# Output projection of a hybrid decoder layer: w_out split once and kept, token tiles one by one

## The chip, the cores and the metric

The kernel runs on one core of one Trainium2 chip. The metric is the device time of one execution, in microseconds (us). Before the change the median of three runs is 1144.28 us (1142.41 the lowest).

## What is computed

One decoder layer on x of 1024 tokens by 1024 features in float32: a token mixer (differential attention in 512 columns, a gated short convolution in the other 512), an output projection with a residual and a LayerNorm, then a gated MLP with a causal convolution of width 3, again with a residual and a LayerNorm. Around the change:

```python
cat = jnp.concatenate([attn_out, conv_out], axis=-1)      # (S, 1024)
mix = jnp.einsum('bsc,cd->bsd', cat, w_out)               # output projection
h = layer_norm(DEEPNORM_ALPHA * h + mix, ln1_g, ln1_b)    # h1
f = conv_glu(h, ffn_w_up, ffn_conv_w, ffn_conv_b, ffn_w_down)
```

## The kernel before

Every float32 matrix product runs in a rounded format: `split` (lines 57 to 64) cuts an operand into a high part (a cast on ACT, line 60) and a low part (a subtraction on DVE, or on POOL where asked, line 61), and `mm3` (66 to 71) issues three matmuls: high by high, high by low, low by high. The gated MLP and the input projections use a scheme of seven block products in place of eight; its seven right-hand operands for the MLP, made of the transposed h1, are `hb` "11", "21", "t1", "t2", "22", "t3" and "t4" (each a high and a low tile of 128 x 4 x 512). "11" and "21" come from tokens 0 to 511, "22" from the others, and t1 to t4 are sums and differences of both halves.

The output projection (lines 578 to 628) works on groups of three, three and two token tiles of 128 tokens (t0 = 0, 3, 6). In a group, the loop over eight k-blocks of 128 rows of w_out loads and splits the k-block (`weights`, 569 to 575: 20 loads of 512 KB in all, since two k-blocks are handed from one group to the next), loads and splits the matching piece of the mixer output `cat_d` (`cr`, `ch`, `cl`, 589 to 593), and issues 18 matmuls into the `op` accumulators (two PSUM banks for each token tile). At the end of a group DVE adds the residual to each tile (613). LayerNorm (`norm`, 615, and `layer_norm`, 514 to 525: statistics on DVE, a reciprocal root on POOL, two 128x1024 passes on DVE), the write of h1 and the eight 128x128 transposes of a tile (`trp`, 530) wait as `pending` and are called in the next group behind the k-blocks named by NORM_AT (lines 606 to 609), so that PE has matmuls ahead of and behind them.

For the tiles of the second half `combine` (543 to 567) takes the transposed tile from PSUM, rebuilds the old operands by adding their two parts on POOL (551), and makes t1, t2, 22, t3 and t4; the last of these is split by POOL. Then four gate blocks f are begun early (641 to 653) with products that need only "11" and "21", and what is left of the second half comes last (660). The pairs of the MLP follow from line 680 on.

The tile framework orders the instructions of each engine: a list scheduler takes the program's order as priority, and buffers of one tag (the eight PSUM banks have one tag, `b`) are handed out in the order in which their first writers stand. Each engine then runs its own list in order, and SP issues all DMAs in order.

Of the kernel before, what the change touches and what calls it, by code (L numbers as in the profile page):

```python
# [8 lines left out]
F32 = mybir.dt.float32  # L9
# [34 lines left out]
def layer_kernel(ctx: ExitStack, tc: tile.TileContext, x, xt, w_in, w_v, lam, vecs, w_out, ln, w_up, w_down, out):  # L44
# [468 lines left out]

    def layer_norm(pl, r, dst, gt, bt):
        st = pl.tile([P, 2, 6], F32, name="st", tag="st", bufs=3)
        for i in range(2):
            V.bn_stats(st[:, i, :], r[:, i * 512:(i + 1) * 512])
        mv = pl.tile([P, 2], F32, name="mv", tag="mv", bufs=3)
        V.bn_aggr(mv, st)
        ve = pl.tile([P, 1], F32, name="ve", tag="ve", bufs=3)  # L520
        G.tensor_scalar(ve, mv[:, 1:2], EPS, None, op0=ALU.add)
        rs = pl.tile([P, 1], F32, name="rs", tag="rs", bufs=3)
        G.tensor_tensor(rs, ve, mhalf, op=ALU.pow)
        V.scalar_tensor_tensor(r, r, mv[:, 0:1], gt, op0=ALU.subtract, op1=ALU.mult)
        V.scalar_tensor_tensor(dst, r, rs, bt, op0=ALU.mult, op1=ALU.add)

    def transposed(src, k0):
        ps = p8.tile([P, 4, P], F32, name="trp", tag="b", bufs=8)
        for j in range(4):
            T.transpose(ps[:, j, :], src[:, (k0 + j) * P:(k0 + j + 1) * P], ident)  # L530
        return ps

    def first_half(src, t):
        ts = slice(t * P, (t + 1) * P)
        for k0, n in ((0, "11"), (4, "21")):
            split(hb[n][0][:, :, ts], hb[n][1][:, :, ts], transposed(src, k0))

    def second_half(src, t):

        b_ = [transposed(src, k0) for k0 in (0, 4)]  # L540
        return lambda: combine(t, *b_)

    def combine(t, b12, b22):
        ts = slice((t - 4) * P, (t - 3) * P)

        def put(n, v, eng=None):
            split(hb[n][0][:, :, ts], hb[n][1][:, :, ts], v, eng=eng)

        def old(n, tag, bufs=1):
            v = cp.tile([P, 4, P], F32, name=f"o{n}", tag=tag, bufs=bufs)  # L550
            G.tensor_tensor(v, hb[n][0][:, :, ts].bitcast(F32), hb[n][1][:, :, ts].bitcast(F32), op=ALU.add)
            return v

        t1 = old("11", "tb0", 2)
        t4 = old("21", "tb2")
        V.tensor_tensor(t1, b12, t1, op=ALU.subtract)
        put("t1", t1)
        t2 = cp.tile([P, 4, P], F32, name="t2", tag="tb1")
        V.tensor_tensor(t2, b22, t1, op=ALU.subtract)
        put("t2", t2)  # L560
        put("22", b22)
        t3 = cp.tile([P, 4, P], F32, name="t3", tag="tb0", bufs=2)
        A.copy(t3, b12)
        V.tensor_tensor(t3, b22, t3, op=ALU.subtract)
        put("t3", t3)
        G.tensor_tensor(t4, t4, t2, op=ALU.subtract)
        put("t4", t4, G)

    def weights(t0, k, eng):
        raw = e0.tile([P, D], F32, name=f"wo{t0}_{k}_r", tag="wg", bufs=NWG)  # L570
        SQ.dma_start(raw, w_out[k * P:(k + 1) * P, :])
        wo = [e0.tile([P, 2, 512], F32R, name=f"wo{t0}_{k}_{d}", tag="ring", bufs=RING[0]) for d in range(2)]
        for d in range(2):
            split(wo[d][:, 0, :], wo[d][:, 1, :], raw[:, d * 512:(d + 1) * 512], eng=eng)
        return wo

    pending, late, held = [], [], {}
    for t0 in (0, 3, 6):
        tt = list(range(t0, min(t0 + 3, NT)))
        w = len(tt) * P  # L580
        acc = {(t, d): bank(f"op{t}_{d}") for t in tt for d in range(2)}
        order = K_ORDER if t0 != 3 else K_ORDER[::-1]
        for ki, k in enumerate(order):
            if ki < REUSE and t0:
                wo = held[k]
            else:
                wo = weights(t0, k, G if ki in POOL_LO and t0 == 6 else None)
            held[k] = wo
            cr = cc.tile([P, 384], F32, name="cr", tag="cr", bufs=4)
            SQ.dma_start(cr[:, :w], cat_d[k][:, t0 * P:t0 * P + w])  # L590
            ch = cc.tile([P, 384], F32R, name="ch", tag="ch", bufs=2)
            cl = cc.tile([P, 384], F32R, name="cl", tag="cl", bufs=2)
            split(ch[:, :w], cl[:, :w], cr[:, :w])
            if ki == 0:
                xr = {}
                for t in tt:
                    xr[t] = cx.tile([P, D], F32, name=f"xr{t}", tag="xr", bufs=4)
                    SQ.dma_start(xr[t], x[t * P:(t + 1) * P, :])
            if ki == 1 and t0 == 0:
                g1 = bcast_row(cp, 0, "g1")  # L600
                b1 = bcast_row(cp, 1, "b1")
            for i, t in enumerate(tt):
                s_ = slice(i * P, (i + 1) * P)
                for d in range(2):
                    mm3(acc[t, d], ch[:, s_], cl[:, s_], wo[d][:, 0, :], wo[d][:, 1, :], ki == 0, ki == 7)
            if pending and ki in NORM_AT:
                pending.pop(0)()
        while pending:
            pending.pop(0)()
        for t in tt:  # L610
            for d in range(2):
                ds_ = slice(d * 512, (d + 1) * 512)
                V.scalar_tensor_tensor(xr[t][:, ds_], xr[t][:, ds_], ALPHA, acc[t, d], op0=ALU.mult, op1=ALU.add)

        def norm(t, r):
            layer_norm(cp, r, r, g1, b1)
            SQ.dma_start(h1_d[t], r)

        def turn(t, r):
            if t < 4:  # L620
                first_half(r, t)
            elif t == 4:
                second_half(r, t)()
            else:
                late.append(second_half(r, t))

        rows_ = [(t, xr[t]) for t in tt]
        pending = [(lambda a=a: (norm(*a), turn(*a))) for a in rows_]
# [25 lines left out]
    wu0 = wload8(NF, "wg", NWG)
    s1 = gp.tile([P, 4, P], F32, name="s1_0", tag="s1", bufs=1)
    V.tensor_tensor(s1, wu0[:, 0:4, :], wu0[:, 4:8, :], op=ALU.add)
    v1 = parts(e0, s1)
    V.tensor_tensor(s1, s1, early[0][0][:, 0:4, :], op=ALU.subtract)
    ready1 = v1, s1, parts(e0, s1)
    for step in late:  # L660
        step()
# [274 lines left out]
```

## Time and profile before

| | us |
|---|---|
| median of the runs | 1144.28 |
| the profiled execution, its own time | 1145.87 |
| its span, first to last instruction | 1143.5 |
| PE busy in the span | 1090.8 |
| DVE busy | 914.4 |
| ACT busy | 522.5 |
| POOL busy | 174.6 |

The busy times say which engine has the most to do over the whole span; what the output projection is worth is read from its own stretch, which runs from 377.28 us (its first matmul) to about 517 us (the pairs of the MLP under way).

### The profile page before, as it was taken

To read this page: it belongs to the slowest core of one execution; us is meant where nothing else is said; L and a number is where in the kernel's file an instruction comes from. 1 tells how busy PE (TensorE), PEld (TensorE's weight loads), DVE (VectorE), ACT (ScalarE), POOL (GpSimd) and SP (SyncE) were. 2 spreads that over 40 slices of the span, in tenths; PEclk is the share of its full clock that TensorE was granted. 3 is DMA by queue.
4 is the path that set the end of the run, shared out by engine and by line. 5 is a ranking of instruction groups with operands and counts; after the bars stand their busy time and mean duration, and the time that the engine had idled before them with its cause. 6 is when DMAs were issued, how large, how long until landed. Compare 5 with 4: busy or idle time off the path is not lost.

```text
span 1143.5 us, 13823 instructions
## 1 busy us (share of the span) xinstructions
PE 1090.8 (95%) x4924; PEld 876.7 (77%) x4924; DVE 914.4 (80%) x1377; ACT 522.5 (46%) x980; POOL 174.6 (15%) x198
## 2 busy tenths in 40 slices
PE   7899999999999999789999999999999999899997
PEld 5676777877768888568888888888888887688885
DVE  7858889779887788998967676767677599977697
ACT  5347677377676334434433434343434243344450
POOL 4501313113032214760000000000000000000102
PEclk9899999999999999999999999999999999999999
DMA  7430121211205764423232222222222393111111
GB/s 257 136 111 26 42 82 41 86 60 47 79 28 172 263 203 164 152 74 111 94 109 75 92 74 93 74 93 73 93 74 74 121 411 139 37 62 40 38 74 73
DMA packets 50276, 118.51 MB, mean 104 GB/s; under 512 B 5024, under 2 KB 18464, under 8 KB 50208
## 3 DMA queue, kind: packets, MB, share of 16 engines
q1 hardware_dynamic: 50208, 117.64, 29.8%
q8 instruction: 38, 0.62, 0.2%
q14 instruction: 30, 0.25, 0.1%
HBM read 90.88 MB, written 26.74 MB: 103 GB/s over the span
## 4 chain that ended last, share of the span: by engine, by line
PE 67%; DVE 17%; ACT 6%; DMA 5%; POOL 3%; issue 2%; POOLq 0%; DVEq 0%; SPq 0%; ACTq 0%
PE X L71 8%; PE X L69 8%; PE X L70 8%; PE Z L70 5%; PE Z L71 5%; PE Z L69 5%; PE dx L70 3%; PE dx L71 3%; PE dx L69 3%; PE op L71 2%; PE op L70 2%; PE op L69 2%; DVE a L61 2%; PE dz L70 2%; PE dz L71 2%
## 5 line engine op out<-in xcount | busy, mean ns | idle before, releaser
L61 DVE TENSOR_TENSOR a<-s,a 128x512 fp32r<-128x512 f32 x118 | 85.4, 725 | 45.1 <-ACT a L60 44.1
L60 ACT CAST a<-s 128x512 fp32r<-128x512 f32 x118 | 73.4, 623 | 94.8 <-PE X L71 42.7
L60 ACT CAST a<-w 128x512 fp32r<-128x512 f32 x106 | 66.0, 623 | 87.4 <-PE X L71 40.7
L61 DVE TENSOR_TENSOR a<-w,a 128x512 fp32r<-128x512 f32 x102 | 71.4, 701 | 21.6 <-ACT a L60 21.2
L60 ACT CAST T<-b 128x512 fp32r<-128x512 f32 x66 | 40.7, 622 | 72.1 <-PE dz L71 35.6
L70 PE MATMUL dx<-T,S 128*128 128x512 f32 x176 | 69.8, 397 | 3.6 <-DVE T L61 3.6
L71 PE MATMUL dx<-T,S 128*128 128x512 f32 x176 | 69.4, 395 | 0.0
L69 PE MATMUL dx<-T,S 128*128 128x512 f32 x176 | 67.3, 390 | 0.0
L61 DVE TENSOR_TENSOR T<-b,T 128x512 fp32r<-128x512 f32 x66 | 45.4, 690 | 24.1 <-ACT T L60 24.1
L687 POOL MEMSET gs<- 128x2 f32 x22 | 2.2, 100 | 379.2 <-DVE t L706 379.2
L71 PE MATMUL op<-wo,cl 128*128 128x512 f32 x128 | 51.4, 402 | 4.5 <-DVE cl L61 4.5
L422 DVE TENSOR_REDUCE nm<-sc 128x1 f32<-128x128 f32 (+5 forms) x64 | 47.6, 751 | 7.6 <-PE sc L421 7.1
L69 PE MATMUL dz<-T,S 128*128 128x512 f32 x132 | 49.2, 401 | 3.8 <-ACT T L60 3.7
L70 PE MATMUL dz<-T,S 128*128 128x512 f32 x132 | 52.2, 396 | 0.0
L71 PE MATMUL dz<-T,S 128*128 128x512 f32 x132 | 51.9, 393 | 0.0
L69 PE MATMUL op<-wo,ch 128*128 128x512 f32 x128 | 51.4, 402 | 0.0
L70 PE MATMUL op<-wo,ch 128*128 128x512 f32 x128 | 51.0, 399 | 0.0
L426 ACT ACTIVATE p<-sc,nm 128x128 f32<-128x128 f32 (+5 forms) x64 | 47.6, 746 | 7.3 <-DVE p L435 4.1
L707 ACT ACTIVATE t<-t 128x1024 f32<-128x1024 f32 x22 | 23.4, 1062 | 51.2 <-DVE t L706 51.2
L344 POOL TENSOR_TENSOR me<-me,y 128x256 f32<-128x256 f32 x16 | 12.6, 786 | 217.9 <-ACT y L343 217.9
L419 PE MATMUL sc<-k,q 128*128 128x512 f32 (+2 forms) x96 | 37.2, 394 | 7.3 <-ACT p L426 6.1
L60 ACT CAST wo<-wo_r 128x512 fp32r<-128x512 f32 x40 | 24.4, 620 | 41.0 <-PE op L71 37.8
(312 smaller groups left out, 3415.3 us busy)
## 6 DMA issues: line engine op xcount, KB each, us to landing
w<-in_w_up SPq DMA_DIRECT2D x44, 512.0 KB, 3.3
b<-in_w_down SPq DMA_DIRECT2D x44, 256.0 KB, 6.8
w<-in_w_in SPq DMA_DIRECT2D x20, 512.0 KB, 3.5
wo_r<-in_w_out SPq DMA_DIRECT2D x20, 512.0 KB, 5.4
act_d<-act SPq DMA_DIRECT2D x19, 512.0 KB, 2.6
ra<-act_d SPq DMA_DIRECT2D x19, 512.0 KB, 7.1
v_d<-vs SPq DMA_DIRECT2D x16, 256.0 KB, 2.7
vhl<-v_d SPq DMA_DIRECT2D x8, 512.0 KB, 4.7
```

What stands on the lines that cost most here:

```text
L60: A.copy(hi, src)
L61: (eng or V).tensor_tensor(lo, src, hi.bitcast(F32), op=ALU.subtract)
L69: T.matmul(ps, lh, rh, start=first, stop=False, **kw)
L70: T.matmul(ps, lh, rl, start=False, stop=False, **kw)
L71: T.matmul(ps, ll, rh, start=False, stop=last, **kw)
L344: G.tensor_tensor(me, me, y, op=ALU.mult)
L419: T.matmul(sc[:, bs], q2[m][:, qs], k2[m][:, bs], start=True, stop=False)
L422: V.tensor_reduce(nm[:, m:m + 1], sc[:, :n], axis=AX.X, op=ALU.max, negate=True)
L426: A.activation(pt[:, :n], sc[:, :n], AF.Exp, bias=nm[:, m:m + 1], accum_out=sm[:, m:m + 1])
L687: G.memset(gs[:, 0:2], 0.0)
L707: A.activation(t_, t_, AF.Silu)
```

## The change

w_out is split once, in passes of 128x1024, into eight tiles that lie in the buffers of the operands t2, 22, t3 and t4, and stays there for all token tiles. The mixer output is split in two halves of 512 columns (`mixer`), whose tiles take the seven ring buffers and one of their own. Token tiles 0 to 2 run together over the k-blocks, then tiles 3 to 7 one by one, 48 matmuls each. Ahead of each of these stands the LayerNorm of the tile before, with its transposes. Operands of the second half are computed by rows, out of h1 as it was written to DRAM (`diff`, `b21`), and then transposed: t1 at once, the four others behind the four early gate blocks. POOL has no splits or sums there any more.

```diff
-POOL_LO = (2, 3, 4, 5, 6)
-REUSE = 2
-NORM_AT = (2, 3, 5)
...
-    def first_half(src, t):
...
-    def weights(t0, k, eng):
...
-    pending, late, held = [], [], {}
-    for t0 in (0, 3, 6):
...
+    def weights(i):
+        k = K_ORDER[i]
+        raw = e0.tile([P, 2, 512], F32, name=f"wo{k}_r", tag="wg", bufs=NWG)
+        SQ.dma_start(raw, w_out[k * P:(k + 1) * P, :].rearrange("p (a b) -> p a b", a=2))
+        tag = f"hb_{LATE_OPS[i // 2]}{'hl'[i % 2]}"
+        w = hop.tile([P, 4, 512], F32R, name=f"wo{k}", tag=tag)
+        split(w[:, 0:2], w[:, 2:4], raw)
+        wo[k] = w
...
+    def rows(t):
+        xr[t] = cx.tile([P, D], F32, name=f"xr{t}", tag="xr", bufs=5)
+        SQ.dma_start(xr[t], x[t * P:(t + 1) * P, :])
+        acc[t] = [bank(f"op{t}_{d}") for d in range(2)]
...
+    def first_half(t):
+        norm(t)
+        put("11", t, transposed(xr[t], 0))
+        put("21", t, transposed(xr[t], 4))
...
+    def second_half(t):
+        r = xr[t]
+        v = cx.tile([P, 512], F32, name=f"diff{t}", tag="diff", bufs=4)
+        SQ.dma_start(v, h1_d[t - 4][:, 0:512])
+        norm(t)
+        V.tensor_tensor(v, r[:, 0:512], v, op=ALU.subtract)
+        put("t1", t, transposed(v, 0))
+        V.tensor_tensor(v, r[:, 512:D], v, op=ALU.subtract)
+        diff[t] = v
+
+    def late(n, t):
+        r = xr[t]
+        if n == "t2":
+            src = diff[t]
+        elif n == "22":
+            src = r[:, 512:D]
+        elif n == "t3":
+            src = r[:, 0:512]
+            V.tensor_tensor(src, r[:, 512:D], src, op=ALU.subtract)
+        else:
+            src = cc.tile([P, 512], F32, name=f"b21_{t}", tag="cr", bufs=3)
+            SQ.dma_start(src, h1_d[t - 4][:, 512:D])
+            V.tensor_tensor(src, src, diff[t], op=ALU.subtract)
+        put(n, t, transposed(src, 0))
+
+    for t in range(3):
+        rows(t)
+    for i in range(NK):
+        weights(i)
+        mixer(i, 0)
...
+        for t in range(3):
+            mms(t, i)
+    for t in range(3, NT):
+        rows(t)
+        if t == 4:
+            for i in range(NK):
+                mixer(i, 1)
+        if t == 3:
+            for u in range(3):
+                first_half(u)
+        elif t == 4:
+            first_half(3)
+        else:
+            second_half(t - 1)
+        for i in range(NK):
+            mms(t, i)
+    second_half(NT - 1)
...
     for f in range(NEARLY):
-        if f >= NEARLY - 2:
-            turn(*rows_[f - NEARLY + 2])
...
+        for t in range(4, NT):
+            late(LATE_OPS[f], t)
```

On PE, before, around the transposes of the first token tile (`trp` is the transposed tile, `xr` the normed rows, `op` an accumulator, `wo` a part of w_out, `ch` and `cl` the parts of the mixer output; the `op` rows are of the second group of tiles):

```order
L71 MATMUL op_0_3956<-wo_6_0_4014,cl 128x512
L69 MATMUL op_1_3957<-wo_6_1_4015,ch 128x512
L70 MATMUL op_1_3957<-wo_6_1_4015,ch 128x512
L71 MATMUL op_1_3957<-wo_6_1_4015,cl 128x512
L530 MATMUL trp<-ident,xr_3694 128x128 x8
L69 MATMUL op_0_3952<-wo_2_0_4072,ch 128x512
L70 MATMUL op_0_3952<-wo_2_0_4072,ch 128x512
L71 MATMUL op_0_3952<-wo_2_0_4072,cl 128x512
```

On PE, changed, at the end of token tiles 0 to 2 (`c` is a split tile of the mixer output; `op_0_3902` belongs to tile 3):

```order
L68 MATMUL op_0_3670<-wo_3874,c_3_3879 128x512
L66 MATMUL op_1_3671<-wo_3874,c_3_3879 128x512
L67 MATMUL op_1_3671<-wo_3874,c_3_3879 128x512
L68 MATMUL op_1_3671<-wo_3874,c_3_3879 128x512
L528 MATMUL trp<-ident,xr_3660 128x128 x8
L528 MATMUL trp<-ident,xr_3664 128x128 x8
L528 MATMUL trp<-ident,xr_3668 128x128 x8
L66 MATMUL op_0_3902<-wo_3674,c_4_3679 128x512
L67 MATMUL op_0_3902<-wo_3674,c_4_3679 128x512
L68 MATMUL op_0_3902<-wo_3674,c_4_3679 128x512
```

The 24 transposes of tiles 0 to 2 now stand directly behind the matmuls that make these tiles and ahead of the first matmul of tile 3. On PE, changed, between tiles 4 and 5 (`op_1_4043` is of tile 4, `diff_4164` is made of its normed rows, `op_0_4162` is of tile 5):

```order
L66 MATMUL op_1_4043<-wo_3874,c_3_4081 128x512
L67 MATMUL op_1_4043<-wo_3874,c_3_4081 128x512
L68 MATMUL op_1_4043<-wo_3874,c_3_4081 128x512
L528 MATMUL trp<-ident,diff_4164 128x128 x4
L66 MATMUL op_0_4162<-wo_3674,c_4_4046 128x512
L67 MATMUL op_0_4162<-wo_3674,c_4_4046 128x512
L68 MATMUL op_0_4162<-wo_3674,c_4_4046 128x512
```

So it stands behind every tile from 3 to 7. On ACT, before, where the stage begins (`me` and `y` belong to the last attention output and follow the matmuls into `mq`):

```order
L60 CAST wo_4_0_3682<-wo_4_r 128x512
L60 CAST wo_4_1_3683<-wo_4_r 128x512
L60 CAST wo_5_0_3720<-wo_5_r 128x512
L60 CAST wo_5_1_3721<-wo_5_r 128x512
L60 CAST ch<-cr 128x384 x2
L60 CAST wo_0_0_3756<-wo_0_r 128x512
L60 CAST wo_0_1_3757<-wo_0_r 128x512
L60 CAST wo_1_0_3788<-wo_1_r 128x512
L340 ACTIVATE me<-mq,epsc 128x256
L342 ACTIVATE y<-me 128x256
L343 ACTIVATE y<-y 128x256
```

On ACT, changed, at the same place:

```order
L57 CAST c_4_3679<-cr 128x512
L57 CAST c_5_3707<-cr 128x512
L57 CAST c_0_3739<-cr 128x512
L337 ACTIVATE me<-mq,epsc 128x256
L57 CAST c_1_3767<-cr 128x512
L339 ACTIVATE y<-me 128x256
L340 ACTIVATE y<-y 128x256
L57 CAST c_2_3795<-cr 128x512
L57 CAST c_6_3823<-cr 128x512
L57 CAST wo_3674<-wo_r 128x1024
L57 CAST wo_3702<-wo_r 128x1024
```

The first cast of w_out, which stood ahead of the operations on `mq`, now stands behind them and behind two casts of the mixer output. DVE has the same change: the first low part of w_out stands behind the convolution's last passes (before: lines 442 to 449) and two low parts of the mixer output.

## Rows read from the trace of the kernel before

**Rows 1.** Windows of core 0: busy us (instructions) by engine, granted clock, DMA share, GB/s

```profile
449.00:482.00 33.00, 26.18 (x115) 19.50 (x114) 32.01 (x38) 16.01 (x32) 27.17 (x20) 0.96 0.47 155
482.00:518.00 36.00, 31.06 (x127) 24.69 (x126) 33.48 (x43) 14.20 (x26) 20.71 (x17) 0.90 0.16 59
518.00:536.00 18.00, 17.89 (x79) 14.50 (x78) 15.12 (x23) 10.36 (x17) 0.10 (x1) 1.00 0.37 124
...
377.28:510.36 133.08, 123.44 (x547) 98.31 (x545) 112.37 (x148) 51.26 (x99) 63.22 (x49) 0.97 0.50 170
510.36:517.55 7.19, 5.06 (x14) 3.52 (x13) 6.50 (x10) 3.45 (x6) 2.87 (x3) 0.76 0.00 0
```

**Rows 2.** What PE waited for from 377 to 518 us: total, times, longest

```profile
PE op L71 <- DVE cl L61: 4.5, 3, 2.3
...
PE trp L530 <- DVE xr L525: 2.2, 1, 2.2
```

**Rows 3.** Timeline of PE: start, us, instruction, [idle before it <- releaser]

```profile
377.28 0.40 PE L69 MATMUL op<-wo,ch 128*128 128x512 f32 x1
...
377.98 0.40 PE L69 MATMUL op<-wo,ch 128*128 128x512 f32 x1
...
423.48 1.03 PE L530 MATMUL trp<-ident,xr 128*128 128x128 f32 x8
424.27 0.48 PE L69 MATMUL op<-wo,ch 128*128 128x512 f32 x1
...
469.49 1.06 PE L530 MATMUL trp<-ident,xr 128*128 128x128 f32 x8 [2.24 <-DVE xr L525]
...
479.40 0.63 PE L70 MATMUL op<-wo,ch 128*128 128x512 f32 x1
...
481.96 0.63 PE L70 MATMUL X<-hb_11l,a 128*128 128x512 f32 x1
```

**Rows 4.** Timeline of PE in the first microseconds of the kernel

```profile
9.66 0.79 PE L69 MATMUL vps<-wv_s,xb_11h 128*128 128x512 f32 x1 [1.37 <-ACT xb_11h L60]
...
14.52 0.61 PE L70 MATMUL vps<-wv_s,xb_11h 128*128 128x512 f32 x1
```

**Rows 5.** Timeline of DVE: residual sums, statistics and the passes of LayerNorm

```profile
479.71 1.87 DVE L613 SCALAR_TENSOR_TENSOR xr<-xr,op 128x512 f32<-128x512 f32 x3
...
482.38 1.87 DVE L517 BATCH_NORM_STATS2 st<-xr 128x6 f32<-128x512 f32 x3
...
484.83 1.27 DVE L524 SCALAR_TENSOR_TENSOR xr<-xr,mv,g 128x1024 f32<-128x1024 f32 x1
486.02 0.20 DVE L519 BATCH_NORM_AGGREGATE mv<-st 128x2 f32<-128x12 f32 x1
...
486.69 2.31 DVE L525 SCALAR_TENSOR_TENSOR xr<-xr,rs,b 128x1024 f32<-128x1024 f32 x1
```

**Rows 6.** Timeline of POOL: the reciprocal root of a LayerNorm

```profile
484.75 0.57 POOL L523 TENSOR_TENSOR rs<-ve,mhalf 128x1 f32<-128x1 f32 x1
```

**Rows 7.** Groups by form: line, engine, operation, count | busy us, mean ns | idle before

```profile
L61 DVE TENSOR_TENSOR wo<-wo_r,wo 128x512 fp32r<-128x512 f32 x24 | 19.6, 822 | 10.8 <-ACT wo L60 10.8
...
L61 DVE TENSOR_TENSOR wv_s<-wv_r,wv_s 128x1024 fp32r<-128x1024 f32 x3 | 3.7, 1226 | 0.8 <-ACT wv_s L60 0.8
L60 ACT CAST wv_s<-wv_r 128x1024 fp32r<-128x1024 f32 x3 | 3.1, 1045 | 0.9 <-DMA wv_r<-in_w_v 0.8
```

**Rows 8.** Timelines of ACT and DVE where the stage begins

```profile
378.44 0.42 ACT L343 ACTIVATE y<-y 128x256 f32<-128x256 f32 x1
...
381.80 0.71 DVE L449 TENSOR_TENSOR w<-p,w 128x512 f32<-128x512 f32 x1
```

**Rows 9.** SP's queue, a window of the DMAs, and DMA groups (KB each, median us to landing)

```profile
391.61 0.33 SPq L590 DMA_DIRECT2D cr<-cat_d  x1
...
391.00:396.00 5.00, 5.00 (x23) 3.99 (x23) 2.56 (x5) 1.56 (x3) 0.00 (x0) 1.00 0.97 369
...
h_d<-xr SPq DMA_DIRECT2D x8, 512.0 KB, 4.0
```

More of the change, by code (lines that the diff above doesn't have):

```diff
@@ L503, in layer_kernel @@
     cp = pool("cp", cp_st, side="right")
-    hb = {n: [hop.tile([P, 4, 512], F32R, name=f"hb_{n}{c}", tag=f"hb_{n}{c}") for c in "hl"] for n in OPS}
+    LATE_OPS = ("t2", "22", "t3", "t4")
+    hb = {}
     def bank(name):
@@ L531, in transposed @@
         return ps
-    def first_half(src, t):
[L534 to L567, printed above, removed]
@@ L569, in weights @@
-    def weights(t0, k, eng):
-        raw = e0.tile([P, D], F32, name=f"wo{t0}_{k}_r", tag="wg", bufs=NWG)
-        SQ.dma_start(raw, w_out[k * P:(k + 1) * P, :])
-        wo = [e0.tile([P, 2, 512], F32R, name=f"wo{t0}_{k}_{d}", tag="ring", bufs=RING[0]) for d in range(2)]
-        for d in range(2):
-            split(wo[d][:, 0, :], wo[d][:, 1, :], raw[:, d * 512:(d + 1) * 512], eng=eng)
-        return wo
-    pending, late, held = [], [], {}
-    for t0 in (0, 3, 6):
[L579 to L628, printed above, removed]
@@ new lines, in put @@
+    def put(n, t, v):
+        if n not in hb:
+            hb[n] = [hop.tile([P, 4, 512], F32R, name=f"hb_{n}{c}", tag=f"hb_{n}{c}") for c in "hl"]
+        ts = slice(t % 4 * P, (t % 4 + 1) * P)
+        split(hb[n][0][:, :, ts], hb[n][1][:, :, ts], v)
+    wo = {}
+    def weights(i):
[6 more added lines that the diff above has]
+        wo[k] = w
@@ new lines, in layer_kernel, with mixer @@
+    cat = {}
+    def mixer(i, half):
+        k = K_ORDER[i]
+        cr = cc.tile([P, 512], F32, name="cr", tag="cr", bufs=3)
+        SQ.dma_start(cr, cat_d[k][:, half * 512:(half + 1) * 512])
+        if i < NK - 1:
+            c = e0.tile([P, 2, 512], F32R, name=f"c{half}_{k}", tag="ring", bufs=RING[0])
+        else:
+            c = cc.tile([P, 2, 512], F32R, name=f"c{half}_{k}", tag="c8")
+        split(c[:, 0], c[:, 1], cr)
+        cat[half, k] = c
+    xr, acc = {}, {}
+    def rows(t):
+        xr[t] = cx.tile([P, D], F32, name=f"xr{t}", tag="xr", bufs=5)
+        SQ.dma_start(xr[t], x[t * P:(t + 1) * P, :])
+        acc[t] = [bank(f"op{t}_{d}") for d in range(2)]
@@ new lines, in mms, with norm @@
+    def mms(t, i):
+        k = K_ORDER[i]
+        c, w, ts = cat[t // 4, k], wo[k], slice(t % 4 * P, (t % 4 + 1) * P)
+        for d in range(2):
+            mm3(acc[t][d], c[:, 0, ts], c[:, 1, ts], w[:, d], w[:, 2 + d], i == 0, i == NK - 1)
+    def norm(t):
+        r = xr[t]
+        for d in range(2):
+            ds_ = slice(d * 512, (d + 1) * 512)
+            V.scalar_tensor_tensor(r[:, ds_], r[:, ds_], ALPHA, acc[t][d], op0=ALU.mult, op1=ALU.add)
+        layer_norm(cp, r, r, g1, b1)
+        SQ.dma_start(h1_d[t], r)
@@ new lines, in first_half @@
+    def first_half(t):
+        norm(t)
+        put("11", t, transposed(xr[t], 0))
+        put("21", t, transposed(xr[t], 4))
+    diff = {}
+    def second_half(t):
[7 more added lines that the diff above has]
+        diff[t] = v
@@ new lines, in late @@
+    def late(n, t):
+        r = xr[t]
+        if n == "t2":
[10 more added lines that the diff above has]
+        put(n, t, transposed(src, 0))
@@ new lines, in layer_kernel @@
+    for t in range(3):
[3 more added lines that the diff above has]
+        mixer(i, 0)
+        if i == 1:
+            g1, b1 = bcast_row(cp, 0, "g1"), bcast_row(cp, 1, "b1")
+        for t in range(3):
[10 more added lines that the diff above has]
+            first_half(3)
+        else:
+            second_half(t - 1)
+        for i in range(NK):
+            mms(t, i)
@@ L631, in layer_kernel @@
+    second_half(NT - 1)
+    for n in LATE_OPS:
+        hb[n] = [hop.tile([P, 4, 512], F32R, name=f"hb_{n}{c}", tag=f"hb_{n}{c}") for c in "hl"]
     early = {}
@@ L639, in wgate @@
         return wload8(f, "wg", NWG)
-    for a in rows_:
-        norm(*a)
     for f in range(NEARLY):
-        if f >= NEARLY - 2:
-            turn(*rows_[f - NEARLY + 2])
         wg, X, Y = wgate(f), bank(f"X{f}"), bank(f"Y{f}")
@@ L649, in layer_kernel @@
         A.copy(p1, X)
-        block_product(e0, Y, None, hb, "21", True, parts(e0, wg[:, 4:8, :], G))
+        block_product(e0, Y, None, hb, "21", True, parts(e0, wg[:, 4:8, :]))
         c11 = gp.tile([P, 512], F32, name=f"c11_{f}", tag="c11", bufs=NEARLY)
@@ L653, in layer_kernel @@
         early[f] = wg, X, c11
[L654 to L661, printed above, removed]
+        if f == NEARLY - 1:
+            wu0 = wload8(NF, "wg", NWG)
+            s1 = gp.tile([P, 4, P], F32, name="s1_0", tag="s1", bufs=1)
+            V.tensor_tensor(s1, wu0[:, 0:4, :], wu0[:, 4:8, :], op=ALU.add)
+            v1 = parts(e0, s1)
+            V.tensor_tensor(s1, s1, early[0][0][:, 0:4, :], op=ALU.subtract)
+            ready1 = v1, s1, parts(e0, s1)
+        for t in range(4, NT):
+            late(LATE_OPS[f], t)
     cp_st.close()
```

## The prediction

> **What bounds the kernel now.** I read the granted clock and the span first, then windows over the stage, then what PE waited for, and last the timelines of PE and DVE at the places that the change moves. Outside the stage PE is full: from 518 to 536 us it is busy 17.89 of 18.00 us, 79 matmuls, 0.2265 us each [rows 1]. So only time in which PE gets through its list slower than that is to be won or lost.
>
> The stage runs from its first matmul at 377.28 to 517.55 us, 133.08 + 7.19 = 140.27 us [rows 1, 3]. What must be done in it: 384 matmuls of the output projection at 0.2333 us (three from 377.28 to 377.98 [rows 3]) = 89.6 us; 96 of the early gate blocks and 13 of the first pair at 0.2265 = 24.7 us; 64 transposes, of which eight and the longer matmul behind them cost 0.87 us (423.48 to 424.27, and 0.48 in place of 0.40 [rows 3]) = 7.0 us. That is 121.3 us, so 19.0 us are lost, nearly all behind 449 us, where PE is busy 26.18 of 33 and 31.06 of 36 us [rows 1]. The reader is to see there that PE waits for low parts of the mixer output (4.5 us) and for the last pass of a LayerNorm (2.2 us) [rows 2], and that behind the waits matmuls come at 0.427 us: seven from 479.40 to 481.96, in a stretch with a mean granted clock under 1 [rows 1, 3], which is the 1.2 GHz level.
>
> **What goes.** w_out is split 16 times (in units of 128x512) and not 40 times, and POOL leaves the stage. At most this gives back the 19.0 us: PE cannot be faster than full. I count it all as gained and enter below what comes in its place.
>
> **More transposes.** t1, t2, 22, t3 and t4 are transposed apart, 16 each for four tiles, so 32 + 80 = 112 in place of 64. 48 more at 0.87 / 8 = 5.2 us.
>
> **The start.** Before, w_out's first parts were ready when PE came from the projections; PE went on at 377.28 without a gap [rows 3]. Now the first cast of w_out stands behind the operations on `mq` and behind casts of the mixer output. The last operation on `mq` ended at 378.86 [rows 8]; with one more cast ahead of it and two behind, about 0.5 us each, ACT begins with w_out at 380.5 and is done at 381.6 (1.045 us [rows 7]). On DVE the low part stands behind the last convolution pass, which ended at 382.5 [rows 8] and now does so at about 381.9, and behind two low parts of 0.6 us: 383.1, and 1.23 us more [rows 7] is 384.3. PE can do two matmuls before that. Loss: 384.3 - 377.28 - 0.5 = 6.5 us. Ends: 4 us if the casts of the mixer output come early, 8 us if one of their loads is late.
>
> Later k-blocks cost nothing if they come in time. The sixth has to wait in SP's queue for the last piece of the convolution: before, the read behind it went out at 391.61 [rows 9]. Behind it now go two pieces of the mixer output, three tiles of x, two rows of LayerNorm and w_out's sixth block, 3.5 MB; at the 369 GB/s of that time [rows 9] it lands at 401 and is split by 404. PE wants it at 384.3 + 5 x 18 x 0.2333 + 2 = 407. At half the rate it would come 6 us late; I take nothing and keep 6 us for the range.
>
> **Behind tiles 0 to 2.** Here the order decides. PE's next rows are 24 transposes, which need three finished LayerNorms, and tile 3's matmuls stand behind them. Before, matmuls of the next group stood on both sides. What DVE has left when the last matmul of tile 2 is issued: some 0.5 us of a residual sum; ten operations on 128x512 (two residual sums, four statistics, four low parts) at 1.87 / 3 = 0.62; two aggregations of 0.2; six passes on 128x1024 at 1.19 (484.83 to 486.02), with POOL idle, for with a split on POOL one took 2.31 [rows 5]. 0.5 + 6.2 + 0.4 + 7.1 = 14.2 us. POOL's root (0.57 us [rows 6]) lies beside the first pass. In that time PE does 16 of the transposes, 1.7 us: 12.5 us are lost.
>
> **Behind tiles 3 to 7.** After tile 3 DVE does one residual sum, two low parts of the mixer output, two statistics, an aggregation and two passes: 0.2 + 5 x 0.62 + 0.2 + 2.4 = 5.9, with the handover 6.0 us. After tiles 4 to 7 the two low parts are not in it, but a subtraction is, the rows minus the old h1 (not in the trace in this form; the residual sum, also on 128x512, is nearest): 0.2 + 0.62 + 1.25 + 0.2 + 2.4 + 0.62 + 0.1 = 5.4 us, four times: 21.6 us. Nothing else is on PE's list in these gaps.
>
> **The clock.** Seven gaps of 5 us and more now stand before a dense stretch: the start, behind tiles 0 to 2, and behind 3, 4, 5, 6 and 7. After a wait of 2.3 us seven matmuls ran at 0.427 us, 1.35 us lost [rows 2, 3]; in the first microseconds of the kernel, after one of 1.37 us, twelve did (9.66 to 14.52 [rows 4]), 2.3 us lost. I take 2.0 us, nearer to the second since these gaps are longer: 14.0 us, with 9.5 and 16 as ends.
>
> **Late operands.** Behind each early gate block stand 16 transposes. DVE has seven operations there (4.3 us) and PE 24 matmuls and the transposes (7.2 us), so PE covers them. Only the last tile's t4 waits: its load of old h1 needs a buffer that the first tile's transposes free, and takes about as long as the write of h1, 4.0 us [rows 9], against some 3.4 us of PE's work; with the subtraction 1.0 us is lost. SP now has h1's writes ahead of the reads of old h1, each waiting for its LayerNorm; what is queued behind (rows of x, old h1) is wanted tiles later, over 15 us.
>
> **Sum.** 6.5 + 12.5 + 6.0 + 21.6 + 14.0 + 1.0 + 5.2 = 66.8 us, less 19.0: +47.8 us. The profiled execution took 1145.87 us (span 1143.5), so 1193.7; the median of the runs is 1.6 us lower: 1192 us.
>
> **Rivals.**
>
> *PE stays full.* If tile t+1's matmuls ran while the LayerNorm of tile t is going on, the gaps behind the tiles and their clock losses would fall away, and -19.0 + 5.2 + 6.5 + 2.0 = -5.3 us would be left: 1139 us, not slower. For it speaks that DVE sheds 24 splits of w_out and runs without POOL's splits, which had stretched a mean low part of w_out to 822 ns [rows 7]. It decides at the first transposes behind tile 2: either a matmul of tile 3 is issued before them or not. Against it: at 469.49 PE sat idle for 2.24 us in front of eight transposes until DVE's pass was done [rows 3], and each tile's LayerNorm takes its first number from the last matmul ahead of the gap, so no faster DVE closes it. I give it 0.04. The Trainium skill ("TensorE: Matmul & The Clock Gate", section "Step-by-step: what each phase is for") says that PE pulls only weight loads ahead and keeps matmuls in program order; by that rule this rival falls, and the idle 2.24 us agree.
>
> *Every stretch runs at the lower clock.* If, with a gap after each 48 matmuls, PE kept the 0.427 us for all of them, tiles 3 to 7 would cost 5 x 48 x 0.193 = 46 us where the sum has 10: 1228 us. For it: behind 449 us waits of some 2 us already brought the mean granted clock to 0.96, 0.90 and 0.76 [rows 1]. Against it: the last row of the slow seven is 2.6 us behind the first [rows 3], and even the kernel's first stretch was slow for some 5 us only [rows 4], less than half of the 11.2 us of a tile. 0.07. The Trainium skill (same page, section "HAM oscillation — how this bites in real kernels") shows a loop whose bursts of some 2 us start cold each time after waits of 3 to 5 us; a tile's stretch is five times as long, so by that page too the beginning alone is slow.
>
> *w_out's late blocks hold PE.* The 6 us above, twice over with the loads of x ahead of them: 1204 us, chance 0.04. Inside the range.
>
> **How the numbers follow.** The forecast, a gap behind each tile, has 0.85, and the rivals 0.04, 0.07 and 0.04. Its own ends: clock 9.5, start 4 and no wait for the last t4 give -8; clock 16, start 8 and 6 us for w_out give +10; durations of the chain on DVE, of some 40 us, 10% either way: 4 more. So 1180 to 1206; I give 1178 to 1210, which leaves out the first two rivals and a little at each end. A measurement of this kernel tells about 2% from no change, 23 us: slower by over 2% has all cases but the first rival and a little of the forecast's low end: 0.94; within 2% 0.05; faster 0.01.
>
> **What would show it.** In the changed kernel's trace: PE idle by some 12 us around its first transposes, with DVE's second pass of a LayerNorm as releaser; five more gaps of 5 to 6 us, about 19 us apart (11.2 of matmuls, 0.5 of transposes, 2 for the clock, 5.4 of waiting); the first matmul of the stage with w_out's low part at about 384; PE busy at some 70% over tiles 3 to 7, with a granted clock below 0.95; the pairs of the MLP 48 us later than before and then as before. The forecast is wrong if matmuls of a next tile stand in front of its predecessor's transposes in the trace, or if the gaps are under 3 us.

## The result, and the profile after

The changed kernel takes 1200.72 us (median; 1197.77 to 1201.74) beside 1144.03 us for the kernel before in the same comparison: ratio 1.0496, 95% interval 1.0469 to 1.0524. It is slower by 5%, inside the predicted range and 9 us above the predicted time. One of the four executions of the kernel before took 2755.74 us; the ratio leaves it out, and the median of the other three is 1143.79 us. The profiled execution took 1199.74 us (span 1198.0), 53.9 us more than that of the kernel before.

All of it lies in the stage of the output projection. The engines are PE (TensorE, the matmuls), DVE (VectorE), ACT (ScalarE) and POOL (GpSimd). The columns of a window are the stretch and its length, the busy us (and instructions) of PE, of PE's weight loads, of DVE, ACT and POOL, then the granted clock, the DMA share and GB/s. The changed kernel over tiles 4 to 7 with the four early gate blocks, over the beginning of the pairs, and over tiles 3 to 7 alone:

```profile
456.00:568.00 112.00, 86.25 (x370) 70.59 (x369) 52.59 (x77) 18.74 (x34) 7.50 (x9) 0.86 0.06 25
568.00:586.00 18.00, 17.55 (x79) 13.90 (x78) 17.24 (x26) 9.17 (x16) 0.10 (x1) 1.00 0.47 162
...
434.00:537.00 103.00, 68.28 (x264) 54.71 (x263) 49.81 (x70) 12.95 (x22) 9.36 (x11) 0.83 0.19 65
```

The second row answers to the last of the three stretches of [rows 1] (518 to 536): 79 matmuls in 18 us here and there, so the pairs run as before. In the first row every engine has time to spare: PE is busy for 77% and DVE for 47%, and the granted clock is 0.86; over tiles 3 to 7 alone it is 66%, 48% and 0.83. No engine is the bound where all of them have slack; what binds is a chain that goes from one to the other and back. What PE waited for from 376 to 575 us (total, times, longest), to be read beside [rows 2]:

```profile
PE trp L528 <- DVE diff L596: 25.8, 4, 6.7
PE trp L528 <- DVE xr L523: 19.6, 4, 9.0
PE op L66 <- ACT wo L57: 4.5, 1, 4.5
PE op L67 <- DVE wo L58: 1.7, 1, 1.7
```

These are ten gaps, 51.6 us. Before, all waits of PE there came to 11.6 us: the two groups of [rows 2], 4.5 and 2.2 us, 2.6 us in shorter ones, and this one:

```profile
PE X L69 <- ACT t L563: 2.3, 1, 2.3
```

The gaps one after the other, in the PE timeline of the changed kernel (start, duration, instruction, in brackets the idle time before it and what ended it); around 475 us some of the matmuls behind a gap are shown too:

```profile
380.27 1.22 PE L66 MATMUL op<-wo,c 128*128 128x512 f32 x2 [4.55 <-ACT wo L57]
383.20 0.80 PE L67 MATMUL op<-wo,c 128*128 128x512 f32 x1 [1.71 <-DVE wo L58]
...
421.78 1.71 PE L528 MATMUL trp<-ident,xr 128*128 128x128 f32 x8 [3.75 <-DVE xr L523]
427.23 1.97 PE L528 MATMUL trp<-ident,xr 128*128 128x128 f32 x8 [3.73 <-DVE xr L523]
432.38 1.97 PE L528 MATMUL trp<-ident,xr 128*128 128x128 f32 x8 [3.18 <-DVE xr L523]
...
454.97 1.94 PE L528 MATMUL trp<-ident,xr 128*128 128x128 f32 x8 [8.97 <-DVE xr L523]
...
475.64 1.08 PE L528 MATMUL trp<-ident,diff 128*128 128x128 f32 x4 [6.40 <-DVE diff L596]
476.38 0.78 PE L66 MATMUL op<-wo,c 128*128 128x512 f32 x1
476.95 0.63 PE L67 MATMUL op<-wo,c 128*128 128x512 f32 x1
477.38 0.63 PE L68 MATMUL op<-wo,c 128*128 128x512 f32 x1
...
480.26 0.40 PE L66 MATMUL op<-wo,c 128*128 128x512 f32 x1
480.50 0.39 PE L67 MATMUL op<-wo,c 128*128 128x512 f32 x1
480.73 0.40 PE L68 MATMUL op<-wo,c 128*128 128x512 f32 x1
```

The pattern of 475.64 comes again at 495.63, 515.89 and 536.70 (6.29, 6.31 and 6.74 us idle). From 476.95 to 479.51 the matmuls start 0.427 us apart, as those at 1.2 GHz in [rows 3]; from 480.26 on 0.24 us and less. The lower level of the clock holds for the first 4 us of each tile's stretch and not for the rest. If every start more than 0.3 us behind the one before it is counted, and what it takes beyond 0.2265 us is added up (for transposes, beyond 0.109 us, which 16 of them take in e1_within where PE is full), the ten gaps cost 20.3 us behind them: 3.3 at the start, 3.8 around the transposes of tiles 0 to 2, 2.4 to 3.1 behind each of tiles 3 to 7 (13.2). Not quite all of it is the clock: in e2_dummy below, where the clock stays up behind tiles 3 to 7, the same count still finds 1.2 us behind five gaps. So some 18 us are the clock.

With that the stage adds up. It runs from 375.7 to 571.5 us, 195.8. The 384 matmuls at 0.227 us (50 of them from 388.26 to 399.61) are 87.2; gate blocks and the first pair's beginning 24.7, as before; transposes 7.0 + 5.2; gaps 51.6; what is lost behind the gaps 20.3; together 196.0.

Why a gap behind a tile is 6.4 us long is read from DVE's timeline between tiles 4 and 5, and POOL's:

```profile
468.57 1.39 DVE L579 SCALAR_TENSOR_TENSOR xr<-xr,op 128x512 f32<-128x512 f32 x2 [10.31 <-PE op L68]
469.88 1.28 DVE L515 BATCH_NORM_STATS2 st<-xr 128x6 f32<-128x512 f32 x2
471.19 0.21 DVE L517 BATCH_NORM_AGGREGATE mv<-st 128x2 f32<-128x12 f32 x1
471.43 1.28 DVE L522 SCALAR_TENSOR_TENSOR xr<-xr,mv,g 128x1024 f32<-128x1024 f32 x1
473.48 1.28 DVE L523 SCALAR_TENSOR_TENSOR xr<-xr,rs,b 128x1024 f32<-128x1024 f32 x1 [0.76 <-POOL rs L521]
474.80 0.69 DVE L596 TENSOR_TENSOR diff<-xr,diff 128x512 f32<-128x512 f32 x1
```

```profile
418.29 0.24 POOL L519 TENSOR_SCALAR ve<-mv 128x1 f32<-128x1 f32 x1 [32.88 <-DVE mv L517]
...
471.49 1.31 POOL L519 TENSOR_SCALAR ve<-mv 128x1 f32<-128x1 f32 x1 [17.98 <-DVE mv L517]
472.88 0.57 POOL L521 TENSOR_TENSOR rs<-ve,mhalf 128x1 f32<-128x1 f32 x1
```

DVE idles 10.31 us for the tile's last matmul and then PE idles for DVE: the two take turns. Inside the chain DVE waits 0.76 us for POOL, whose addition of one number to each row takes 1.31 us here and 0.24 us at 418.29.

### The profile page after: what moved, and what is told of

The parts are those of the page before. It is cut to its first block, busy times and chain, and to the rows that moved or that the text cites. A ratio compares the mean times of both kernels' runs of the same rounds, so it can differ in the third digit from the quotient of the medians.

```text
span 1198.0 us, 13747 instructions
## 1 busy us (share of the span) xinstructions
PE 1104.2 (92%) x4972; PEld 889.0 (74%) x4972; DVE 898.3 (75%) x1359; ACT 505.3 (42%) x936; POOL 128.0 (11%) x168
## 4 chain that ended last, share of the span: by engine, by line
PE 52%; DVE 7%; DMA 4%; POOL 1%; issue 1%; ACT 0%; SPq 0%; POOLq 0%; DVEq 0%; ACTq 0%
PE X L66 7%; PE X L67 7%; PE X L68 7%; PE Z L66 3%; PE Z L68 3%; PE Z L67 3%; PE dx L67 3%; PE dx L68 3%; PE dx L66 2%; PE Y L68 2%; PE dz L68 2%; PE dz L67 2%; PE Y L67 2%; PE Y L66 2%; PE dz L66 2%; DMA h_d<-xr 1%
## 5 line engine op out<-in xcount | busy, mean ns | idle before, releaser
L58 DVE TENSOR_TENSOR a<-w,a 128x512 fp32r<-128x512 f32 x106 | 74.8, 705 | 28.9 <-ACT a L57 28.4
L66 PE MATMUL op<-wo,c 128*128 128x512 f32 x128 | 55.3, 434 | 4.5 <-ACT wo L57 4.5
L67 PE MATMUL op<-wo,c 128*128 128x512 f32 x128 | 53.9, 421 | 1.7 <-DVE wo L58 1.7
L68 PE MATMUL op<-wo,c 128*128 128x512 f32 x128 | 53.7, 419 | 0.0
L717 ACT ACTIVATE t<-t 128x1024 f32<-128x1024 f32 x22 | 23.4, 1062 | 47.8 <-DVE t L716 47.8
L67 PEld LDWEIGHTS dx<-T,S 128*128 128x128 f32 x176 | 33.4, 190 | 11.9 <-DVE T L58 4.9
L66 PEld LDWEIGHTS dx<-T,S 128*128 128x128 f32 x176 | 33.3, 189 | 7.5 <-ACT T L57 0.6
```

The costliest lines, as they stand in the source:

```text
L717: A.activation(t_, t_, AF.Silu)
```

## The experiments

The theory: the time is lost because, in PE's program order, each tile's transposes stand directly behind its own matmuls, so that PE waits through a whole LayerNorm, and then pays again in clock. The rivals: DVE, the splits of w_out, the loads or the extra transposes would cost the time in any order; or the clock costs little.

**e1_within.** Each tile's LayerNorm and transposes are called inside the matmuls of the next tile, the last tile's behind the first gate block (so that the transposes of its t2 stand one gate block later too). Nothing else is changed: the same instructions, splits and loads.

```diff
+    DUE = {3: {2: (0,), 6: (1,)}, 4: {1: (2,), 5: (3,)}, 5: {5: (4,)}, 6: {5: (5,)}, 7: {5: (6,)}}
     for t in range(3, NT):
...
-        if t == 3:
-            for u in range(3):
-                first_half(u)
-        elif t == 4:
-            first_half(3)
-        else:
-            second_half(t - 1)
         for i in range(NK):
             mms(t, i)
+            for u in DUE[t].get(i, ()):
+                (first_half if u < 4 else second_half)(u)
-    second_half(NT - 1)
...
-        for t in range(4, NT):
+        if f == 0:
+            second_half(NT - 1)
+        for t in range(4, NT - 1 if f == 0 else NT):
             late(LATE_OPS[f], t)
+        if f == 1:
+            late(LATE_OPS[0], NT - 1)
```

> The changed kernel, but each tile's LayerNorm and transposes stand among the matmuls of the next tile (behind its third to seventh k-block) and tile 7's behind the first gate block; everything else as changed. Theory (the order makes the gaps, and the gaps lower the clock): of the changed trace's 51.6 us of waits in the stage the 10.7 behind tiles 0 to 2, the 9.0 behind tile 3 and the 25.7 behind tiles 4 to 7 go, and most of some 17 us at the lower clock with them; the start (6.3 us) and 48 transposes stay: about 1200 - 45 - 13 = 1142 us, PE idle under 5 us between 384 us and the pairs. Rival (DVE, ACT or the loads bound the tiles and the order only shows it): waits turn up among the matmuls in place of the gaps, and the time stays above 1180 us.

Measured: 1145.37 us, ratio 1.001 (1.000 to 1.002). PE's waits from 376 to 530 us, and the window that stands above for the changed kernel:

```profile
PE op L66 <- ACT wo L57: 3.8, 1, 3.8
PE op L67 <- DVE wo L58: 2.4, 1, 2.4
PE trp L528 <- DVE xr L523: 2.3, 3, 1.6
PE trp L528 <- DVE diff L596: 2.3, 1, 2.3
```

```profile
456.00:568.00 112.00, 109.25 (x517) 89.34 (x516) 91.99 (x136) 42.76 (x73) 6.23 (x10) 1.00 0.21 80
```

45.4 us of waiting for LayerNorms have become 4.6, and in the same stretch of time 517 matmuls stand where 370 did (from 514.5 us on those of the pairs), at a full clock. So 55 of the 57 us came from the order alone: the calls move a tile's LayerNorm on DVE and POOL and its write of h1 along with the transposes, but not what has to be done. The time is 3 us above the expectation, which had no waits for LayerNorms left; the four short waits are of that size.

**e2_dummy.** Behind the matmuls of each of tiles 3 to 7, ahead of its transposes, 24 more matmuls into a bank of their own, whose result nobody reads. The gaps are filled with work of no use.

```diff
+    def keep(t):
+        ps = bank(f"kp{t}")
+        c, w = cat[t // 4, K_ORDER[NK - 1]], wo[K_ORDER[NK - 1]]
+        for j in range(24):
+            T.matmul(ps, c[:, 0, t % 4 * P:(t % 4 + 1) * P], w[:, j % 2], start=j == 0, stop=j == 23)
...
+        keep(t)
```

> The changed kernel with 24 more matmuls behind each of tiles 3 to 7, into a PSUM bank that nobody reads; they take 24 x 0.2333 = 5.6 us of PE in gaps of 6.3 to 9.0 us. The chain on DVE is the same. Theory (the clock falls because PE is idle, and costs about 2 us behind each gap): PE's clock stays up in tiles 4 to 7 and the kernel gets faster by 5 x 2 = 10 us, to about 1190 us, though it does 120 matmuls more. Rival (the matmuls behind a gap are slow for another reason, such as a load or the weights): no faster than the changed kernel, 1200 us, or slower if the added matmuls delay the transposes.

Measured: 1187.74 us, ratio 1.0382 (1.0366 to 1.0397): 13.0 us faster than the changed kernel with 120 matmuls more. PE between tiles 4 and 5, and the window again:

```profile
466.69 5.76 PE L620 MATMUL kp<-wo,c 128*128 128x512 f32 x24
473.18 0.66 PE L528 MATMUL trp<-ident,diff 128*128 128x128 f32 x4 [0.72 <-DVE diff L596]
473.59 0.48 PE L66 MATMUL op<-wo,c 128*128 128x512 f32 x1
```

```profile
456.00:568.00 112.00, 107.99 (x509) 88.04 (x508) 62.98 (x93) 24.54 (x45) 7.53 (x9) 1.00 0.13 48
```

Behind tiles 3 to 7 the gaps and the added matmuls take 6.0 + 27.2 = 33.2 us where the gaps alone took 34.7. What is saved is mainly the clock: counted as above, 1.2 us are lost behind these gaps and not 13.2. 1.5 + 12.0 = 13.5 us answer to the 13.0 measured, so the clock is shown to cost time apart from the gaps.

**e3_act_root.** The reciprocal root of the LayerNorm is made by ACT (a logarithm and an exponential) and not by POOL.

```diff
-        G.tensor_scalar(ve, mv[:, 1:2], EPS, None, op0=ALU.add)
+        A.activation(ve, mv[:, 1:2], AF.Ln, bias=epsc)
-        G.tensor_tensor(rs, ve, mhalf, op=ALU.pow)
+        A.activation(rs, ve, AF.Exp, scale=-0.5)
```

> The changed kernel with the reciprocal root of the first LayerNorm on ACT (Ln, then Exp with scale -0.5) in place of POOL. Theory (POOL's addition is held while DVE's first pass runs, so that the second pass waits 0.75 us for the root): the 0.75 us wait ahead of the second pass goes in tiles 3 to 7, the gaps fall from 6.4 to about 5.65 us, 5 x 0.75 = 3.8 us in all: about 1197 us. Rival (the wait is the handover itself): ACT's two operations and handovers take as long, no change within 1 us.

Measured: 1196.69 us, ratio 1.046 (1.0441 to 1.0478), 4.0 us below the changed kernel (the runs of the two just overlap, 1194.88 to 1198.34 and 1197.77 to 1201.74; the profile shows the cause more directly). DVE's two passes now stand 0.12 us apart and the four gaps behind tiles 4 to 7 are 2.6 us shorter (25.8 before):

```profile
470.15 1.28 DVE L522 SCALAR_TENSOR_TENSOR xr<-xr,mv,g 128x1024 f32<-128x1024 f32 x1
471.55 1.29 DVE L523 SCALAR_TENSOR_TENSOR xr<-xr,rs,b 128x1024 f32<-128x1024 f32 x1
```

```profile
PE trp L528 <- DVE diff L596: 23.2, 4, 6.1
```

**e4_cat_early.** The pieces of the mixer output for the second half are loaded into the buffers of w_out's loads, which stand empty, and not into the three `cr` buffers.

```diff
+        if half:
+            if i % 2 == 0:
+                crs.append(e0.tile([P, 2, 512], F32, name=f"cr{i}", tag="wg", bufs=NWG))
+            cr = crs[-1][:, i % 2, :]
...
```

> The changed kernel with the second half of the mixer output loaded into the buffers of the w_out and gate weights, all eight pieces before the first LayerNorm's write of h1 is waited for, and not through three small buffers. Theory (tile 3's gap is 9.0 us and not 6.4 since the last two pieces land late and DVE's statistics stand behind their low parts): the gap behind tile 3 falls to about 6.5 us, time 1198 us. Rival (the two low parts themselves lengthen it): it stays above 8 us.

Measured: 1198.44 us, ratio 1.048 (1.0459 to 1.0501). The gap behind tile 3 fell from 8.97 to 6.71 us. The time fell by 2.3 us as well, but its runs spread from 1195.01 to 1199.95 us, so that the time by itself would not show it. By the profile, 2.3 us of that gap were low parts of the mixer output that came late and stood ahead of the LayerNorm on DVE.

**e6_start and e5_within_start.** The first two k-blocks of w_out go into four ring buffers and four pieces of the mixer output into two buffers of t2 in their place, so that w_out's first cast can stand ahead of the operations on `mq`; e6_start is the changed kernel with this alone, e5_within_start is e1_within with it (transposes of tiles 0 to 3 one k-block later, those of tile 7 behind the second gate block).

```diff
+        if i < 2:
+            w = [e0.tile([P, 2, 512], F32R, name=f"wo{k}{c}", tag="ring", bufs=RING[0]) for c in "hl"]
+            split(w[0], w[1], raw)
...
-        if i < NK - 1:
+        if i < 3:
             c = e0.tile([P, 2, 512], F32R, name=f"c{half}_{k}", tag="ring", bufs=RING[0])
+        elif i < NK - 1:
+            if i % 2:
+                two[half, i] = hop.tile([P, 4, 512], F32R, name=f"c{half}_{k}", tag=f"hb_t2{'hl'[i // 2 - 1]}")
+            c = two[half, i - 1 + i % 2][:, 2 - i % 2 * 2:4 - i % 2 * 2]
```

> The changed kernel with the buffers of e5_within_start alone; the order behind the tiles is the changed kernel's. Theory: the start's gap of 6.3 us and some 2 us of the clock behind it go: 1200.7 - 8 = about 1192 us. Rival (the wait moves to the third k-block or is hidden by the gaps that follow): 1198 us or more.

> As e1_within, with the first two k-blocks of w_out in ring buffers and four tiles of the mixer output in their place, so that the first split of w_out can be made while the projections still run; the transposes of tiles 0 to 3 are one k-block later, those of tile 7 behind the second gate block. Theory (the stage loses by PE's gaps and by the clock behind them): the gap of 6.3 us at the start with some 2 us of the clock, and 4.6 us of waits at transposes, go: 1145.4 - 8 - 4 = about 1133 us, faster than both kernels. Rival (DVE, which then has the splits of w_out and the convolution's last passes in the same time, is the bound there, and PE waits for the third k-block instead): 1141 us or more.

Measured: e6_start 1198.36 us, ratio 1.0484 (1.0458 to 1.0509); e5_within_start 1140.66 us, ratio 0.9982 (0.9970 to 0.9995). PE goes from the projections into the stage without a gap in both, so the start's 6.3 us and its clock are gone, but only 2.4 us (within the spread of the runs) and 4.7 us of them show in the time. The theory's numbers, 1192 and 1133 us, did not come out. The rivals' times did, 1198 or more for the one and, but for 0.3 us, 1141 or more for the other; not their wait at the third k-block, which is in neither profile, but what e6_start's rival named second, that the gaps that follow hide the gain. The time went into the gap ahead of the first transposes, 3.75 us in the changed kernel, 11.0 in e6_start and 6.5 in e5_within_start, where e1_within had 0.3. PE's longest waits in e6_start, and the row of DVE's timeline that stands right ahead of tile 0's residual sums:

```profile
PE trp L528 <- DVE xr L523: 25.3, 4, 11.0
```

```profile
415.23 0.69 DVE L675 TENSOR_TENSOR s<-w 128x512 f32<-128x512 f32 x1 [10.11 <-DMA w<-in_w_up]
```

It is a sum over a block of w_up that is not needed before the pairs, and it waits 10.1 us for its load, and all LayerNorms with it. In the changed kernel the same instruction waited until 414.40, which cost little there, as the tiles themselves came late.

**e7_within_start_act.** e5_within_start with ACT's root, the edit of e3_act_root.

> e5_within_start with the reciprocal root as a logarithm and an exponential on ACT, so that DVE's second pass no longer waits 0.75 us for POOL. Theory (DVE's chain lies beside matmuls now): the same as e5_within_start within 2 us. Rival (DVE is the bound behind the tiles): 4 us or more below it.

Measured: 1141.54 us, ratio 0.9981 (0.9969 to 0.9992), the same as e5_within_start within 1 us. Where DVE's chain has matmuls beside it, POOL's delay costs nothing that these runs can tell.

**e9_start_s1 and e8_within_start_s1.** The early sum `s1` takes the buffer of `p1`, which binds it to the end of the gate blocks.

```diff
-            s1 = gp.tile([P, 4, P], F32, name="s1_0", tag="s1", bufs=1)
+            s1 = gp.tile([P, 4, P], F32, name="s1_0", tag="p1", bufs=1)
```

> e6_start with the same one buffer changed, the order behind the tiles being the changed kernel's. Theory: the first gap at the transposes falls from 11.0 us to 4 to 5 us, 1198.4 - 6.5 = about 1192 us, so that the start's loss is worth 8 us in the changed kernel once nothing takes its place. Rival: the gap stays as long, as the LayerNorms of tiles 0 to 2 need that time on DVE, 1197 us or more.

> e5_within_start with one buffer changed: s1, a sum over a block of w_up for the first pair, takes the buffer of p1, so that it stands on DVE behind the gate blocks and no longer, waiting 10.9 us for its load, ahead of tile 0's residual sums. Theory (that wait has taken over what the start gave): the 6.5 us gap at the first transposes and some 2 us of the clock behind it go: 1140.7 - 8.5 = about 1132 us. Rival (DVE is late there by its own work, or by the loads of x): 1139 us or more.

Measured: e9_start_s1 1195.26 us, ratio 1.0451 (1.0428 to 1.0474); e8_within_start_s1 1136.78 us, ratio 0.9938 (0.9920 to 0.9956). The gap at the first transposes fell to 3.42 us in the one and vanished in the other, as expected, and a part was lost again. PE's waits in e8_within_start_s1, and DVE's list there:

```profile
PE trp L528 <- DVE b L622: 3.9, 1, 3.9
PE trp L528 <- DVE xr L523: 2.0, 2, 1.6
```

```profile
499.62 0.69 DVE L670 TENSOR_TENSOR s<-w 128x512 f32<-128x512 f32 x1
...
502.63 0.68 DVE L672 TENSOR_TENSOR s<-s,w 128x512 f32<-128x512 f32 x1
503.23 0.69 DVE L622 TENSOR_TENSOR b<-b,diff 128x512 f32<-128x512 f32 x1
```

Now `s1` and its splits stand ahead of the subtraction for the last tile's t4, for which PE waits. The 3.9 us cost another 2.7 us in clock. The same wait of 3.9 us stands in e9_start_s1, with 1.7 us of clock behind it; that more than covers the 3 us by which this run misses its expectation.

**e11_within_start_s1b.** e8_within_start_s1 with two buffers for `p1` and `s1`, so that `s1` stands one gate block earlier.

> e8_within_start_s1 with two buffers for p1 and s1, so that s1 and its splits stand on DVE behind the third gate block and no longer ahead of the last tile's t4. Theory (the wait of 3.9 us before the last transposes came from that order on DVE): it goes, with some 1 us of the clock: 1136.8 - 5 = about 1132 us. Rival (the last tile's t4 waits for its load of old h1 all the same): 1135 us or more.

Measured: 1130.83 us, ratio 0.9892 (0.9874 to 0.9909): faster than the kernel before by 1.1% and than the changed one by 5.8%. All that PE waited for from 376 to 530 us, and the window from its first matmuls to the pairs:

```profile
PE trp L528 <- DVE xr L523: 2.5, 2, 1.6
```

```profile
376.00:520.00 144.00, 141.44 (x677) 117.05 (x676) 113.49 (x164) 44.59 (x77) 19.49 (x23) 1.00 0.45 160
```

So the plan of the change (w_out kept, tile by tile, sums by rows) costs 57 us with the transposes behind their own tiles, and gains 13 once they, w_out's first two k-blocks and `s1` are placed so that PE's list stays full.

## Why the prediction was right, and where its sizes were off

*What goes (19.0 us), More transposes (5.2).* Not measured apart. Together they say -13.8 us for a stage without gaps; e11_within_start_s1b, with 2.5 us of waits left, is at -12.9 against the kernel before in the same comparison. The reading of the profile before left out PE's 2.3 us of waiting for ACT; as the term takes all that PE lost, the sum is the same.

*The start (6.5).* Right: 4.55 + 1.71 = 6.3 us, with the named operations as releasers and the first use of the low part at 383.20 (384 predicted). The later k-blocks of w_out cost nothing, as taken: no other wait for `wo` stands among PE's waits.

*Behind tiles 0 to 2 (12.5).* 3.75 + 3.73 + 3.18 = 10.7 us; smaller, because the transposes between the waits ran slowly (1.97 us for eight, where 0.87 was taken) and so filled more of DVE's chain.

*Behind tiles 3 to 7 (6.0 + 21.6).* The mechanism is right and the size was 7 us short: 8.97 + 25.7 = 34.7. The step said "POOL's root (0.57 us [rows 6]) lies beside the first pass", for tiles 0 to 2, and took the two passes as 2.4 us here too. The root does not lie beside the pass: it waits for POOL's addition, which ends with the pass, and the second pass comes 0.76 us late. e3_act_root takes that away: 2.6 us over the four gaps behind tiles 4 to 7, and 0.6 of the fifth, where DVE's wait fell from 0.74 to 0.12 us. (The fifth gap fell by 1.9 us in all; the rest is no gain of the root, as tile 3's matmuls ended 1.2 us later in that run while the last low part of the mixer output stood at the same time, 449.28 and 449.35 us.) Behind tile 3 the late pieces of the mixer output are the other part, 2.3 us by e4_cat_early. What is left, some 1.6 us over four gaps, fits the last residual sum, which ends 0.7 us behind a tile's last matmul where the step took 0.2; no run changes it.

*The clock (14.0, ends 9.5 and 16).* Mis-sized as well: 20.3 us by the count above, some 18 of them the clock, beyond its upper end either way. The step took 2.0 us for each of seven gaps, from the start of the kernel; five of them cost 2.4 to 3.1, and the other two groups, which are two and three gaps in a row, 3.3 and 3.8. That it is the clock and not the gaps is shown by e2_dummy. The step's first figure came from one wait of 2.34 us (ahead of 478.04); behind the wait of 2.24 us in [rows 3] (ahead of 469.49) no matmul was slow, so that the price of a single gap was less sure than the step had it.

*Late operands (1.0).* Nothing: no wait for `b` stands in the changed kernel's profile. It is there in e8_within_start_s1 and e9_start_s1, by DVE's order and not by the load that the step named.

The errors (-0.2, -1.8, +7.1, +6.3, -1.0, and -2.4 since matmuls ran at 0.227 us and not 0.2333) sum to 8.0 us; the stage grew by 195.8 - 140.3 = 55.5 where 47.8 was forecast. In part they cancel: two terms were 13.4 us too small and the others 5.4 too large. Without those 5.4 the time would still lie in the range. The time of the whole grew by 1.6 us less, as the stage began earlier.

*The rivals.* "PE stays full" fell at the place that was named: no matmul of tile 3 is issued ahead of the first transposes. e1_within makes its condition true, and gives 1145 where it said 1139. Of the 6 us, 4.6 are the short waits, and some 1.4 the clock at the start, 3.4 us where 2.0 was taken; behind the short waits the clock stayed up. One number that spoke for this rival was misread: before, DVE made 30 and POOL 10 of the 40 low parts of w_out, and DVE now makes 16 (8 of 128x1024), so that DVE shed 14 of them and not 24. "Every stretch runs at the lower clock" fell at 480.26 us: some ten of a tile's 48 matmuls are slow. The Trainium skill ("TensorE: Matmul & The Clock Gate", section "HAM oscillation — how this bites in real kernels") tells of a loop in which each burst starts cold; the trace agrees for the beginning of each stretch. "w_out's late blocks hold PE" has no wait in the profile. PE was busy for 66% over tiles 3 to 7 (some 70% forecast) at a clock of 0.83 (below 0.95), the gaps came 20.0 to 20.8 us apart (19), and the pairs ran 54 us later (48).

## What to carry to other kernels

Where a matmul engine and a vector engine hand a tile back and forth, put the next tile's matmuls between a tile and its transposes; a reuse that saves splits and loads can cost more than it saves if it takes that cover away, as it did here. Price a gap with the clock behind it: here 6.4 us of waiting cost 9, and useless matmuls in the gap were cheaper than the gap. When a gap is closed, look at what stands ahead of the waiting instruction on its engine: here the time went twice into one early operation that nobody needed yet, which first waited for its load and then stood in the way.

## What the runs showed of the hardware

POOL's addition on 128x1 takes 0.24 and 0.21 us at 418.29 and 423.13, and 1.30 to 1.31 us in the six other tiles, where it starts within 0.1 us behind DVE's pass of 1.28 us (471.43 and 471.49 above) and ends with it. That pass reads two operands of 128x1024 from SBUF, the rows and `g`. The Trainium skill ("SBUF — State Buffer", section "Who interferes with whom") says that a DVE instruction with two SBUF inputs contends with a GpSimd instruction that reads SBUF, that the port pair they share is an exclusive lock, and that the order of issue decides which of the two is blocked. The trace agrees for these six additions. It agrees also for the 1.27 against 2.31 us of [rows 5]: there POOL's low part began first, at 486.17, ran until 487.93, and the pass that began at 486.69 took 1.04 us longer. It does not agree where POOL's operation is short and only just first: the root at 418.61 (0.57 us) began 0.05 us ahead of DVE's pass at 418.66, and the pass took 1.28 us all the same.

What a gap costs in clock does not follow from its length alone. In e1_within PE idled for 2.30 us ahead of 491.13, and the clock behind it stayed at its upper level; in e5_within_start it idled for 2.09 us ahead of 443.60, and the clock fell to the lower one, 1.2 GHz:

```profile
493.00:497.00 4.00, 4.00 (x19) 3.28 (x18) 3.10 (x6) 1.93 (x4) 0.00 (x0) 1.00 0.00 0
...
443.60:446.00 2.40, 2.40 (x10) 2.30 (x11) 2.33 (x4) 1.03 (x2) 0.00 (x0) 0.51 1.00 367
```

In both, PE had been at work without a longer break ahead of the wait, and why the one differs from the other stays open. By the count above, the gap of 3.87 us costs 2.7 us in e8_within_start_s1 and 1.7 in e9_start_s1, and the gaps from 5.6 to 9.0 us in the changed kernel and the runs with its order cost 1.4 to 3.2 us, the longest of them, 8.97 us, no more than one of 6.40 (2.4 and 2.5). Waits under 0.9 us behind tiles 4 to 6 in e2_dummy cost at most 0.3.
